# Within-chunk products of an SSD mixer: two heads in one PSUM bank instead of one

## The chip, the cores and the metric

The kernel runs on one core of one Trainium2 chip, as one program. The metric is the device time of an execution in microseconds (us). The core has a matrix engine (TensorE, PE in the profile; its weight loads are PEld), a vector engine (VectorE, DVE), an activation engine (ScalarE, ACT), a general engine (GpSimd, POOL) and a queue for transfers (SyncE, SP). Each engine takes its instructions strictly in the order of its program; engines wait for one another by semaphores.

## What is computed

Two layers of an encoder on 512 tokens of width 1024, in float32. Each layer has a mixing part (a pooling mixer, a bidirectional Mamba-2 mixer called SSD, gates, an output projection) and a gated feed-forward part. The change concerns the SSD mixer, cut from the reference to what matters:

```python
SSD_HEADS = 32; SSD_HEAD_DIM = 64; SSD_GROUPS = 4; SSD_STATE = 128; SSD_CHUNK = 128

def ssd_scan(xh, dt, a, bmat, cmat):            # one direction
    ...
    a_cum = jnp.cumsum(jnp.moveaxis(adt, 2, -1), axis=-1)
    seg = a_cum[..., :, None] - a_cum[..., None, :]
    decay = jnp.exp(jnp.where(lower, seg, -jnp.inf))
    scores = jnp.einsum('bclgn,bcsgn->bcgls', cc, bc)
    y_diag = jnp.einsum('bcghls,bcsghp->bclghp', scores[:, :, :, None] * decay, x)
    ...                                          # y_off: the states carried between chunks
    y = y_diag + jnp.moveaxis(y_off, 0, 1)

def bidirectional_ssd(...):
    y_f = ssd_scan(xh, dt[:, :, 0], a[0], bmat, cmat)
    y_b = fl(ssd_scan(fl(xh), fl(dt[:, :, 1]), a[1], fl(bmat), fl(cmat)))
    y = y_f + y_b + d_skip[:, None] * xh
```

The two directions of a head are summed as matrices: `exp` of the masked forward and backward segments, added, times the scores of the group, is one 128x128 matrix per chunk and head, and that matrix times the tokens of the head is `y_diag` of both directions.

## The kernel before, in words

**The main stream.** TensorE's order is written out in the program. Its main work is projections of the 512 tokens with streamed weights. Every float32 weight block is cut into two parts (`wh`, by a cast on ACT, line 90; `wl`, the rest, by a subtraction on DVE, line 91), and every product is three matmuls (lines 298 to 300, in `mm3`). The `wh` and `wl` tiles have three slots each, so a new block can be cast only when TensorE has finished with the block three before it. A projection writes a bank of PSUM from a pool of four (`bank_a`, tiles named `bc`, `xp`, `zp`, `up`, `g0p`, `spp` and so on).

**The background jobs.** The SSD mixer's small matmuls are generators (`Background`): after every few matmuls of the main stream, `bg.tick()` lets one of them put a piece of work into TensorE's order. They use a second pool of four banks (`bank_b`: `xt`, `btp`, `scp`, `stp`, `yop`, `ydp`, `ytp`). A bank is written again only when all that read it are done. The order on the other engines is made by a scheduler from the order in which the instructions were recorded and their priorities; the weights' casts have high priority.

**Units and groups.** Channels of SSD come in 8 units of 256 (4 heads each), 2 units to a group. A group `g` makes B and C (`bc`, then `bt` and `ct`, by a depthwise convolution: ACT reads the bank first, line 389, then DVE reads it four times, line 395, then a SiLU on ACT), their transposes and scores (`scp`, `sct`). A unit `u` makes its convolved tokens (`xp`, `xc`, transposed into `xtok`), its gate (`zp`, `zs`), the states (`stp`, `s`), the products with the states (`yop`, scaled into `yo` by DVE, added to `y` by POOL). When the unit's heads are done, `zs` takes `y`; after the second unit of a group the result is normalised, transposed (`ytp`), cut in two parts on ACT and DVE (`yth`, line 916; `ytl`, line 917), and projected (`spp`).

**The heads.** `heads_job` goes through the 32 heads. `decay(h)` issues a transfer of the two directions' cumulated rows from DRAM to all partitions on ACT's queue (line 756, tile `m`, 128x2x512), masks them on POOL (line 761), takes 8 exponentials of 128x128 on ACT (line 768) and adds the directions on DVE (line 769). Three `m` tiles are in flight. Then the head's matrix is multiplied by the scores on DVE (line 779), 8 matmuls with 64 columns of tokens each (line 786; each is two records in the profile) fill half of a bank `ydp`, and DVE adds it to `y` (line 792). Then `decay(h + 3)` is recorded.

Of the kernel before, what the change touches and what calls it, by code (L numbers as in the profile page):

```python
# [9 lines left out]
F32 = mybir.dt.float32  # L10
# [3 lines left out]
ALU = mybir.AluOpType  # L14
# [3 lines left out]
P = 128  # L18
T = 512
D = 1024  # L20
KD = D // P
NCH = T // P
# [3 lines left out]
ALPHA = (2 * NL) ** 0.25  # L26
EPS = 1e-5
# [9 lines left out]


class WeightStream:
    """Weights in the order in which TensorE takes them: a float32 block is loaded, then cut  # L40
    into two float32r parts whose sum is the block."""

    def __init__(self, nc, tc, pool, plan, ahead, raw_bufs, bufs):
        self.nc, self.tc, self.pool = nc, tc, pool
# [65 lines left out]


class Background:
    """Small pieces of TensorE work, put between the matmuls of the projections: one piece at
    most per tick; a piece says after how many ticks its successor's data can be there."""

    def __init__(self):
        self.jobs = []
# [104 lines left out]
def tile_hybrid_pool_ssd_convffn_encoder(  # L222
# [24 lines left out]
    nc = tc.nc  # L247
# [29 lines left out]
    after = triangle("after", -1, 1, -1)  # L277
# [63 lines left out]
    xq = []  # L341

    def feature_tiles(name, n):
        """n column tiles [128 features, 512 tokens] of the next weights times x."""
        tiles = []
        for i in range(n):
            wh, wl = ws.get()
            ps = bank_a(f"{name}{i}")
            for k in range(KD):
                mm3(ps[: wh.shape[2], :], wh[:, k, :], wl[:, k, :], xts["h"][:, k, :],  # L350
                    xts["l"][:, k, :], k == 0, k == KD - 1)
                if k % 2:
                    bg.tick()
            tiles.append(ps)
        return tiles

    def first_tiles(name, n, fresh=False):
        """The same, by halves of the tokens, with what is left of x's transposes in between."""
        tiles = [bank_a(f"{name}{i}") for i in range(n)]

        def transpose_to(left):
            while len(xq) > left:
                done = xq.pop(0)()
            return done

        got = [ws.get(0)] if fresh else []
        with ExitStack() as order:
            for ins in (last_load, *transpose_to(5)) if fresh else transpose_to(5):
                order.enter_context(tc.issue_after(ins.ins))
            got += [ws.get() for _ in range(n - len(got))]  # L370
        for t0, before in (
            (0, {(0, n - 1): 4, (1, n - 2): 2, (1, n - 1): 1}), (256, {(0, n - 1): 0})
        ):
            for k0 in (0, 4):
                for i in range(n):
                    if (k0 // 4, i) in before:
                        transpose_to(before[k0 // 4, i])
                    wh, wl = got[i]
                    t = slice(t0, t0 + 256)
                    for k in range(k0, k0 + 4):  # L380
                        mm3(tiles[i][: wh.shape[2], t], wh[:, k, :], wl[:, k, :],
                            xts["h"][:, k, t], xts["l"][:, k, t], k == 0, k == KD - 1)
                    bg.tick()
        return tiles

    def conv(dst, ps, taps, bias):
        """Centred depthwise convolution along the tokens; taps are per-feature columns."""
        mid = len(taps) // 2
        nc.scalar.activation(dst, ps, AF.Identity, bias=bias, scale=taps[mid])  # L389
        for j, tap in enumerate(taps):  # L390
# [7 lines left out]
            )  # L398

    def rsqrt(pool, v, name):  # L400
        """v ** -0.5 of positive columns: a guess from the bits, then Newton's iteration."""
        n = v.shape[1]
        i = pool.tile([P, n], I32, tag="rsi", name=f"rsi{name}", bufs=2)
        t = pool.tile([P, n], F32, tag="rst", name=f"rst{name}", bufs=2)
# [7 lines left out]
        return y  # L412

    def token_projection(l, name, src_h, src_l, kn, xcs, lnp, gt, bt, finish, final=False):
        """x <- LayerNorm(ALPHA * x + src @ w), token-major, by chunks of 128 tokens."""
        sts = []
        for c in range(NCH):
            n = 4 if final and c == NCH - 1 else 2
# [4 lines left out]
        warm = lnp.tile([P, 1], F32, tag="warm", name=f"warm{name}")  # L423

        def root(c, mv):
            """(variance + EPS) ** -0.5, with a step of Newton's iteration."""
            v = mv[:, 1:2]
            r = lnp.tile([P, 3], F32, tag="root", name=f"root{name}{c}", bufs=2)
            y, t = r[:, 0:1], r[:, 1:2]
# [5 lines left out]
            return y  # L435

        def pieces(half, c):
            """The columns of a half that are summed and finished together."""
            if final and half == 1 and c == NCH - 1:
                return [slice(0, 256), slice(256, 512)]  # L440
            return [slice(0, 512)]
# [91 lines left out]
            nc.gpsimd.memset(edge[:, gi, 1, t : t + 1], 1.0 / (w - t))  # L533

    for l in range(NL):
        # per-feature parameters as columns
        fw = ffn_conv_w[l].rearrange("j (t p) -> (j t) p", p=P)
        prows = [
            param_rows("pcw", [ssd_conv_w[l].rearrange("j (t p) -> (j t) p", p=P)]),
# [204 lines left out]
        heads_done = [0]  # L744

        def heads_job():
            """The masked decay matrices of the heads, both directions, and the products with
            them within the chunks of 128 tokens."""
            while not dts:
                yield 0  # L750
            nac = dts["nac"]
            ms = {}

            def decay(h):
                m = sp.tile([P, 2, T], F32, tag="m", name=f"m{l}_{h}", bufs=3)
                nc.scalar.dma_start(
                    m, acd[l].rearrange("(d h) t -> d h t", d=2)[:, h, :].partition_broadcast(P)
                )
                for d in range(2):
                    mv = m[:, d].rearrange("p (c t) -> p c t", c=NCH)  # L760
                    nc.gpsimd.affine_select(  # L761
                        out=mv, in_=mv, pattern=[[0, NCH], [1 - 2 * d, P]],
                        compare_op=ALU.is_ge, fill=NEG, base=0, channel_multiplier=2 * d - 1,
                    )
                    for c in range(NCH):
                        mc = m[:, d, c * P : (c + 1) * P]
                        col = d * 32 + h
                        nc.scalar.activation(mc, mc, AF.Exp, bias=nac[:, c, col : col + 1])  # L768
                nc.vector.tensor_tensor(m[:, 0], m[:, 0], m[:, 1], op=ALU.add)  # L769
                ms[h] = (m, bg.now)  # L770

            for h in range(3):
                decay(h)
            for h in range(32):
                u, hh = h // 4, h % 4
                m, start = ms.pop(h)
                while u // 2 not in grp or u not in ytiles or bg.now < start + (6 if h else 7):
                    yield 0
                nc.vector.tensor_tensor(m[:, 0], m[:, 0], grp[u // 2][2], op=ALU.mult)
                yield 2  # L780
                xtok, y = ytiles[u]
                ps = bank_b(f"ydp{l}_{h}")
                for c in range(NCH):
                    for q in range(2):
                        t0 = c * P + q * 64
                        nc.tensor.matmul(
                            ps[q * 64 : (q + 1) * 64, c * 64 : (c + 1) * 64],
                            lhsT=m[:, 0, t0 : t0 + 64],
                            rhs=xtok[:, c, hh * 64 : (hh + 1) * 64], start=True, stop=True,
                        )  # L790
                yv = y[:, :, hh * 64 : (hh + 1) * 64]
                nc.vector.tensor_tensor(
                    yv, yv, ps[:, :256].rearrange("p (c q) -> p c q", c=NCH), op=ALU.add
                )
                heads_done[0] = h + 1
                if h + 3 < 32:
                    decay(h + 3)
                yield 1

        def unit_job(u, xtok, zs, xjobs):  # L800
# [378 lines left out]
```

## Time and profile before

| | |
|---|---|
| runs of the kernel (3) | 1989.05 to 1992.81 us, median 1991.07 us |
| profiled execution, first to last instruction (span) | 1990.3 us |
| TensorE (PE) | 1954.0 us busy, 98% of the span, 10614 records |
| DVE | 1179.1 us busy, 59% |
| ACT | 947.9 us busy, 48% |
| POOL | 430.9 us busy, 22% |
| mean granted TensorE clock | 0.994 of full speed |

The span of the profiled execution lies 0.8 us under the median of the runs, so times of the profile can be set against the runs without a correction. TensorE's matmuls are pipelined: a matmul's record is longer than the distance to the next one's start, so what a piece of work costs TensorE is read from starts, not from durations. In the rows below, `x16` counts merged records, and the bracket at the end of a row gives the idle time of the engine ahead of it and what ended it. The layers are alike: layer 0's mixing part ends near 475 us, layer 1 begins near 995 us and repeats it.

### The profile page before, as it was taken

Reading aid. Unit: us, or ns where it says so; the run is one execution under the profiler, and the core shown is the slowest. Engines: PE = TensorE matmul, PEld = TensorE weight load, DVE = VectorE, ACT = ScalarE, POOL = GpSimd, SP = SyncE. Lnnn points to the kernel's source line nnn. Section 1 sums busy time; section 2 is a strip of 40 time slices with the busy share of each in tenths; the row PEclk is TensorE's granted clock in tenths of the full one; section 3 lists DMA queues with packets and bytes.
Section 4 is the critical chain, followed back from the end, with each engine's and each line's share of the span. In section 5 each row is a group of like instructions: output and inputs, shape, how many; then the busy total and the mean of one; then the engine's idle time right before and its main releaser. Section 6 shows DMA issues by size and latency. Waiting matters only on the chain.

```text
span 1990.3 us, 27038 instructions
## 1 busy us (share of the span) xinstructions
PE 1954.0 (98%) x10614; PEld 1643.9 (83%) x10614; DVE 1179.1 (59%) x1796; ACT 947.9 (48%) x1629; POOL 430.9 (22%) x456
## 2 busy tenths in 40 slices
PE   8999999999999999999999999999999999999998
PEld 7878798988888888888888888989888888888886
DVE  5568576775556655543475685667656566555334
ACT  4767666644332544431257776656443334444321
POOL 1344424241111111110003344252411111111000
PEclk9999999999999999999999999999999999999999
DMA  5443424233241323232325434443333413322321
GB/s 159 127 116 116 127 92 141 85 112 114 79 162 51 106 94 110 94 128 92 97 93 154 115 112 118 116 120 104 90 111 91 169 43 106 106 85 92 129 89 72
DMA packets 172160, 214.87 MB, mean 108 GB/s; under 512 B 6752, under 2 KB 127748, under 8 KB 172032
## 3 DMA queue, kind: packets, MB, share of 16 engines
q1 hardware_dynamic: 151376, 170.14, 26.9%
q10 hardware_dynamic: 17712, 34.08, 6.5%
q0 software_dynamic: 2944, 8.91, 1.4%
q8 instruction: 84, 1.38, 0.3%
q14 instruction: 44, 0.36, 0.1%
HBM read 208.66 MB, written 4.46 MB: 107 GB/s over the span
## 4 chain that ended last, share of the span: by engine, by line
PE 86%; issue 7%; ACT 2%; DVE 2%; POOL 1%; DMA 1%; SPq 0%; ACTq 0%; POOLq 0%; DVEq 0%
PE fg L300 7%; PE fg L299 7%; PE fg L298 7%; PE dp L298 4%; PE dp L299 4%; PE dp L300 4%; PE spp L298 3%; PE spp L299 3%; PE spp L300 3%; PE zp L298 3%; PE zp L299 3%; PE zp L300 3%; PE xp L298 2%; PE xp L299 2%; PE xp L300 2%
## 5 line engine op out<-in xcount | busy, mean ns | idle before, releaser
L91 DVE TENSOR_TENSOR wl<-wraw,wh 128x1024 fp32r<-128x1024 f32 (+1 forms) x318 | 395.8, 1246 | 394.9 <-ACT wh L90 393.6
L90 ACT CAST wh<-wraw 128x1024 fp32r<-128x1024 f32 (+1 forms) x318 | 328.4, 1035 | 434.2 <-PE dp L300 121.9
L300 PE MATMUL fg<-xthm,wl 128*128 128x512 f32 x640 | 249.0, 389 | 0.0
L298 PE MATMUL fg<-xthm,wh 128*128 128x512 f32 x640 | 249.0, 389 | 0.0
L299 PE MATMUL fg<-xtlm,wh 128*128 128x512 f32 x640 | 249.0, 389 | 0.0
L768 ACT ACTIVATE m<-m,nac 128x128 f32<-128x128 f32 x512 | 158.5, 389 | 53.1 <-POOL m L761 52.8
L1122 POOL TENSOR_TENSOR cvv<-cvv,cg 128x512 f32<-128x512 f32 x44 | 56.6, 1286 | 412.8 <-DVE cvv L395 382.0
L299 PEld LDWEIGHTS fg<-xtlm,wh 128*128 128x128 f32 x640 | 120.2, 188 | 25.0
L298 PEld LDWEIGHTS fg<-xthm,wh 128*128 128x128 f32 x640 | 120.2, 188 | 24.9
L300 PEld LDWEIGHTS fg<-xthm,wl 128*128 128x128 f32 x640 | 120.2, 188 | 24.8
L298 PE MATMUL dp<-wh,ah 128*128 128x512 f32 (+1 forms) x352 | 136.6, 388 | 0.0
L300 PE MATMUL dp<-wh,al 128*128 128x512 f32 (+1 forms) x352 | 136.4, 387 | 0.0
L299 PE MATMUL dp<-wl,ah 128*128 128x512 f32 (+1 forms) x352 | 136.4, 387 | 0.0
L761 POOL TENSOR_SCALAR_AFFINE_SELECT m<-m 128x512 f32<-128x512 f32 x128 | 95.0, 767 | 179.6 <-DMA m<-acd 136.8
L298 PE MATMUL spp<-yth,wh 128*128 128x512 f32 x256 | 110.3, 431 | 0.5 <-ACT yth L916 0.5
L876 POOL TENSOR_TENSOR y<-y,yo 128x256 f32<-128x256 f32 x96 | 85.9, 904 | 103.0 <-DVE yo L868 100.2
L299 PE MATMUL spp<-ytl,wh 128*128 128x512 f32 x256 | 101.2, 395 | 0.7 <-DVE ytl L917 0.7
L300 PE MATMUL spp<-yth,wl 128*128 128x512 f32 x256 | 101.1, 395 | 0.0
L395 DVE SCALAR_TENSOR_TENSOR xc<-xp,pcwc,xc 128x510 f32<-128x510 f32 (+1 forms) x128 | 95.2, 745 | 7.7 <-ACT xc L389 6.1
L1125 ACT CAST ah<-cvv 128x512 fp32r<-128x512 f32 x44 | 27.3, 621 | 147.2 <-POOL cvv L1122 147.2
L512 POOL TENSOR_TENSOR x<-x,lnb 128x512 f32<-128x512 f32 x15 | 20.2, 1345 | 325.7 <-DVE x L508 316.1
L769 DVE TENSOR_TENSOR m<-m 128x512 f32<-128x512 f32 x64 | 45.8, 716 | 64.2 <-ACT m L768 54.9
(347 smaller groups left out, 4779.1 us busy)
## 6 DMA issues: line engine op xcount, KB each, us to landing
wraw<-in_w_in_dram SPq DMA_DIRECT2D x56, 1024.0 KB, 5.5
wraw<-in_w_up_dram SPq DMA_DIRECT2D x44, 1024.0 KB, 5.1
m<-acd ACTq DMA_DIRECT2D x64, 512.0 KB, 4.9
wraw<-in_w_down_dram SPq DMA_DIRECT2D x20, 1024.0 KB, 5.1
wraw<-in_w_ssd_proj_dram SPq DMA_DIRECT2D x16, 1024.0 KB, 5.1
wraw<-in_w_in_dram SPq DMA_DIRECT2D x16, 512.0 KB, 5.5
wraw<-in_w_out_dram SPq DMA_DIRECT2D x8, 1024.0 KB, 5.3
xi<-in_x_dram SPq DMA_DIRECT2D x4, 512.0 KB, 6.9
```

The source lines that it names most:

```text
L90: self.nc.scalar.copy(hv, src)
L91: self.nc.vector.tensor_tensor(lv, src, hv, op=ALU.subtract)
L298: nc.tensor.matmul(ps, lhsT=ah, rhs=bh, start=first, stop=False)
L299: nc.tensor.matmul(ps, lhsT=ah, rhs=bl, start=False, stop=False)
L300: nc.tensor.matmul(ps, lhsT=al, rhs=bh, start=False, stop=last)
L395: nc.vector.scalar_tensor_tensor(dst[:, o0:o1], ps[:, o0 + s : o1 + s], tap, dst[:, o0:o1], op0=ALU.mult, op1=ALU.add,)
L761: nc.gpsimd.affine_select(out=mv, in_=mv, pattern=[[0, NCH], [1 - 2 * d, P]], compare_op=ALU.is_ge, fill=NEG, base=0, channel_multiplier=2 ...
L768: nc.scalar.activation(mc, mc, AF.Exp, bias=nac[:, c, col : col + 1])
L769: nc.vector.tensor_tensor(m[:, 0], m[:, 0], m[:, 1], op=ALU.add)
L876: nc.gpsimd.tensor_tensor(y[:, c, :], y[:, c, :], yo[:, d, :], op=ALU.add)
L1122: nc.gpsimd.tensor_tensor(cv, cv, cg, op=ALU.mult)
L1125: nc.scalar.copy(h, cv)
```

## The change

Heads are taken in pairs. A decay tile is made per direction: `m` (forward, four slots) and `mb` (backward, two slots), each 128x512 with a transfer of its own, so that a head has two transfers of 256 KB instead of one of 512 KB. Four heads are prepared ahead instead of three. A pair's two matrices are multiplied by the scores, then 16 matmuls (32 records) fill all 512 columns of one bank, and one addition takes the bank into `y`. Then the next pair but one is prepared. The pauses in ticks are 3 after the multiplications (2 before) and 9 instead of 7 for the first head. The diff also drops docstrings and one comment, which leave empty lines. Its core:

```diff
             def decay(h):
-                m = sp.tile([P, 2, T], F32, tag="m", name=f"m{l}_{h}", bufs=3)
-                nc.scalar.dma_start(
-                    m, acd[l].rearrange("(d h) t -> d h t", d=2)[:, h, :].partition_broadcast(P)
-                )
-                for d in range(2):
-                    mv = m[:, d].rearrange("p (c t) -> p c t", c=NCH)
+                m = sp.tile([P, T], F32, tag="m", name=f"m{l}_{h}", bufs=4)
+                mb = sp.tile([P, T], F32, tag="mb", name=f"mb{l}_{h}", bufs=2)
+                for d, t in enumerate((m, mb)):
+                    col = d * 32 + h
+                    nc.scalar.dma_start(t, acd[l][col : col + 1, :].partition_broadcast(P))
+                    mv = t.rearrange("p (c t) -> p c t", c=NCH)
                     nc.gpsimd.affine_select(
                         out=mv, in_=mv, pattern=[[0, NCH], [1 - 2 * d, P]],
                         compare_op=ALU.is_ge, fill=NEG, base=0, channel_multiplier=2 * d - 1,
                     )
                     for c in range(NCH):
-                        mc = m[:, d, c * P : (c + 1) * P]
-                        col = d * 32 + h
+                        mc = t[:, c * P : (c + 1) * P]
                         nc.scalar.activation(mc, mc, AF.Exp, bias=nac[:, c, col : col + 1])
-                nc.vector.tensor_tensor(m[:, 0], m[:, 0], m[:, 1], op=ALU.add)
+                nc.vector.tensor_tensor(m, m, mb, op=ALU.add)
                 ms[h] = (m, bg.now)
 
-            for h in range(3):
+            for h in range(4):
                 decay(h)
-            for h in range(32):
+            for h in range(0, 32, 2):
                 u, hh = h // 4, h % 4
-                m, start = ms.pop(h)
-                while u // 2 not in grp or u not in ytiles or bg.now < start + (6 if h else 7):
+                (m0, _), (m1, start) = ms.pop(h), ms.pop(h + 1)
+                while u // 2 not in grp or u not in ytiles or bg.now < start + (6 if h else 9):
                     yield 0
-                nc.vector.tensor_tensor(m[:, 0], m[:, 0], grp[u // 2][2], op=ALU.mult)
-                yield 2
+                for m in (m0, m1):
+                    nc.vector.tensor_tensor(m, m, grp[u // 2][2], op=ALU.mult)
+                yield 3
                 xtok, y = ytiles[u]
                 ps = bank_b(f"ydp{l}_{h}")
-                for c in range(NCH):
-                    for q in range(2):
-                        t0 = c * P + q * 64
-                        nc.tensor.matmul(
-                            ps[q * 64 : (q + 1) * 64, c * 64 : (c + 1) * 64],
-                            lhsT=m[:, 0, t0 : t0 + 64],
-                            rhs=xtok[:, c, hh * 64 : (hh + 1) * 64], start=True, stop=True,
-                        )
-                yv = y[:, :, hh * 64 : (hh + 1) * 64]
+                for j, m in enumerate((m0, m1)):
+                    for c in range(NCH):
+                        for q in range(2):
+                            t0 = c * P + q * 64
+                            nc.tensor.matmul(
+                                ps[q * 64 : (q + 1) * 64,
+                                   c * P + j * 64 : c * P + (j + 1) * 64],
+                                lhsT=m[:, t0 : t0 + 64],
+                                rhs=xtok[:, c, (hh + j) * 64 : (hh + j + 1) * 64],
+                                start=True, stop=True,
+                            )
+                yv = y[:, :, hh * 64 : (hh + 2) * 64]
                 nc.vector.tensor_tensor(
-                    yv, yv, ps[:, :256].rearrange("p (c q) -> p c q", c=NCH), op=ALU.add
+                    yv, yv, ps.rearrange("p (c q) -> p c q", c=NCH), op=ALU.add
                 )
-                heads_done[0] = h + 1
-                if h + 3 < 32:
-                    decay(h + 3)
+                heads_done[0] = h + 2
+                for n in (h + 4, h + 5):
+                    if n < 32:
+                        decay(n)
                 yield 1
```

The change moves instructions on every engine but SP, because the scheduler orders ACT, DVE and POOL anew and the jobs fall on other ticks. From the first head pair on, the heads stand earlier among the background pieces. Three places follow. The numbers behind a tile's name are group or unit, then head or column tile.

On ACT in layer 0, around the reading of the bank `bc_1_0` by the convolution of group 1's B (`bt_1`): before,

```order
L90 CAST wh_1143<-wraw_1141 128x1024
L768 ACTIVATE m_3_992<-m_3_992,nac_709 128x128 x2
L768 ACTIVATE m_4_1044<-m_4_1044,nac_709 128x128 x8
L756 DMA m_5_1102<-acd_89 128x2x512
L389 ACTIVATE bt_1_1126<-bc_1_0_975,pcbc,pcwc 128x512
L389 ACTIVATE ct_1_1133<-bc_1_1_1065,pcbc,pcwc 128x512
L756 DMA m_6_1177<-acd_89 128x2x512
L90 CAST wh_1223<-wraw_1141 128x1024
```

and in the changed kernel

```order
L767 ACTIVATE m_6_1156<-m_6_1156,nac_709 128x128 x4
L759 DMA mb_7_1176<-acd_89 128x512
L767 ACTIVATE mb_6_1157<-mb_6_1157,nac_709 128x128 x4
L767 ACTIVATE m_7_1175<-m_7_1175,nac_709 128x128 x2
L90 CAST wh_1363<-wraw_1361 128x1024
L767 ACTIVATE m_7_1175<-m_7_1175,nac_709 128x128 x2
L767 ACTIVATE mb_7_1176<-mb_7_1176,nac_709 128x128 x4
L389 ACTIVATE bt_1_1194<-bc_1_0_1005,pcbc,pcwc 128x512
L389 ACTIVATE ct_1_1201<-bc_1_1_1099,pcbc,pcwc 128x512
```

The reading of `bc_1_0` stood behind the exponentials of head 4 and two casts ahead of `wh_1275`, the cast that takes the slot freed by the last matmul of `xp_2_1` (the column tile of TensorE's stream right ahead of `zp_2_0`); now it stands behind the exponentials of head 7 and behind that same cast, which is `wh_1363` here, with 6 exponentials in between. In both kernels `zp_2_0` writes the bank that `bc_1_0` had.

On ACT in layer 0, around the reading of the first transposed result of group 0 (`ytp_0_0`) by the cut into `yth_0`: before,

```order
L90 CAST wh_1999<-wraw_1997 128x512
L768 ACTIVATE m_12_1871<-m_12_1871,nac_709 128x128 x5
L768 ACTIVATE m_13_1928<-m_13_1928,nac_709 128x128 x8
L736 ACT_TABLE_LOAD
L736 ACTIVATE zs_3_1620<-zp_3_0_1631 128x512
L736 ACTIVATE zs_3_1620<-zp_3_1_1741 128x512
L916 ACTIVATE yth_0_1679<-ytp_0_0_1958,pcbc 128x512
L90 CAST wh_2080<-wraw_2078 128x1024
```

and in the changed kernel

```order
L90 CAST wh_2021<-wraw_1962 128x1024
L767 ACTIVATE m_14_1905<-m_14_1905,nac_709 128x128 x3
L767 ACTIVATE mb_14_1906<-mb_14_1906,nac_709 128x128 x4
L767 ACTIVATE m_15_1924<-m_15_1924,nac_709 128x128 x4
L767 ACTIVATE mb_15_1925<-mb_15_1925,nac_709 128x128 x4
L736 ACT_TABLE_LOAD
L736 ACTIVATE zs_3_1720<-zp_3_1_1839 128x512
L920 ACTIVATE yth_0_1639<-ytp_0_0_1975,pcbc 128x512
```

On TensorE the four transposes `ytp_0` stood between matmuls of `up_0_1` and `g0p_0_0`, with other pieces among them; now all four stand in `up_0_0`, with 6 matmuls after each of the first three, and the next background piece is `xt_3_0`, 12 matmuls behind the fourth. `xt_3_0` writes the bank of `ytp_0_0` again. The cast `wh_2021` waits for the last use of the first part of `up_0_0`'s weights.

On DVE in layer 0, in the changed kernel, ahead of the scaling of `yop_1_1` into `yo_1_1`:

```order
L91 TENSOR_TENSOR wl_1368<-wraw_1361,wh_1367 128x1024
L395 SCALAR_TENSOR_TENSOR xc_2_1_1353<-xp_2_1_0_1270,pcwc,xc_2_1_1353 128x510
L395 SCALAR_TENSOR_TENSOR xc_2_1_1353<-xp_2_1_0_1270,pcwc,xc_2_1_1353 128x511
L91 TENSOR_TENSOR wl_1568<-wraw_1565,wh_1567 128x1024
L395 SCALAR_TENSOR_TENSOR xc_2_1_1353<-xp_2_1_0_1270,pcwc,xc_2_1_1353 128x511
L768 TENSOR_TENSOR m_10_1437<-m_10_1437,mb_10_1438 128x512
L395 SCALAR_TENSOR_TENSOR xc_2_1_1353<-xp_2_1_0_1270,pcwc,xc_2_1_1353 128x510
L768 TENSOR_TENSOR m_11_1456<-m_11_1456,mb_11_1457 128x512
L872 TENSOR_TENSOR yo_1_1_1579<-yop_1_1_1578,ef_704 128x512
```

Here `yop_1_1` and `yop_1_2`, which follow each other on TensorE 6 matmuls apart, have been given the same bank (in the kernel before they had two different ones), so `yop_1_2` waits for this `yo_1_1`, and `yo_1_1` for the addition of head 11, whose last exponential stands 18 instructions behind the first one of head 10 on ACT.

## Rows read from the trace of the kernel before

**Rows 1.** The page, part 1: busy time, share, instructions

```profile
PE 1954.0 (98%) x10614; PEld 1643.9 (83%) x10614; DVE 1179.1 (59%) x1796; ACT 947.9 (48%) x1629; POOL 430.9 (22%) x456
```

**Rows 2.** TensorE's waits, whole span: us in total, times, longest us

```profile
PE stp L835 <- POOL xw L818: 6.5, 4, 2.1
PE g0p L298 <- ACT zs L736: 3.0, 2, 1.9
...
PE ydp L786 <- ACT m L768: 0.8, 2, 0.4
PE spp L299 <- DVE ytl L917: 0.7, 2, 0.4
```

**Rows 3.** Timeline of TensorE around a head's products: start us, us, instruction

```profile
87.28 0.39 PE L300 MATMUL bc<-xthi,wl 128*128 128x512 f32 x1
87.60 0.69 PE L786 MATMUL ydp<-xtok,m 128*64 128x64 f32 x16
...
88.55 0.39 PE L299 MATMUL bc<-xtli,wh 128*128 128x512 f32 x1
```

**Rows 4.** Timeline of TensorE around four and eight transposes in a row

```profile
15.89 0.60 PE L305 MATMUL xtpi<-ident,xi 128*128 128x128 f32 x4
...
16.44 0.28 PE L299 MATMUL dbc<-xtli,wh 128*128 128x256 f32 x1
...
19.20 1.03 PE L305 MATMUL xtpi<-ident,xi 128*128 128x128 f32 x8
...
20.19 0.28 PE L299 MATMUL dbc<-xtli,wh 128*128 128x256 f32 x1
```

**Rows 5.** The tile m: duration ns min/median/max, and landing times

```profile
L761 POOL TENSOR_SCALAR_AFFINE_SELECT m<-m x128: 629/636/1715, 71.0 to 1418.6; 128x512 f32<-128x512 f32 x128
...
DMA to landing us min/median/max: 4.5/4.9/9.5
```

**Rows 6.** Timeline of ACT, 60 to 130 us

```profile
78.07 0.37 ACTq L756 DMA_DIRECT2D m<-acd  x1
78.09 3.31 ACT L768 ACTIVATE m<-m,nac 128x128 f32<-128x128 f32 x11
...
115.56 1.04 ACT L90 CAST wh<-wraw 128x1024 fp32r<-128x1024 f32 x1
```

**Rows 7.** Timeline of ACT, 104 to 106 us

```profile
104.79 0.76 ACT L389 ACTIVATE bt<-bc,pcbc,pcwc 128x512 f32<-128x512 f32 x1
```

**Rows 8.** Timeline of TensorE at the end of xp_2_1 and the start of zp_2_0

```profile
114.96 0.39 PE L299 MATMUL xp<-xtli,wh 128*128 128x512 f32 x1
...
115.41 0.28 PE L298 MATMUL zp<-wh,xthi 128*128 128x256 f32 x1
```

**Rows 9.** Timeline of DVE at the convolution of group 1's B and C

```profile
107.54 0.74 DVE L395 SCALAR_TENSOR_TENSOR bt<-bc,pcwc,bt 128x510 f32<-128x510 f32 x1
108.20 0.73 DVE L395 SCALAR_TENSOR_TENSOR ct<-bc,pcwc,ct 128x510 f32<-128x510 f32 x1
```

**Rows 10.** Groups by form on ACT: busy us, mean ns | idle before

```profile
L916 ACT ACTIVATE yth<-ytp,pcbc 128x512 fp32r<-128x512 f32 x32 | 20.9, 694 | 10.7 <-PE ytp L911 10.7
L736 ACT ACTIVATE zs<-zp 128x512 f32<-128x512 f32 x32 | 18.8, 593 | 1.8 <-PE zp L300 1.5
...
L736 ACT ACT_TABLE_LOAD x12 | 15.4, 1283 | 0.2
```

**Rows 11.** Groups by form on DVE: the same columns

```profile
L917 DVE SCALAR_TENSOR_TENSOR ytl<-ytp,pcbc,yth 128x512 fp32r<-128x512 f32 x32 | 23.4, 746 | 5.6 <-ACT yth L916 5.6
```

**Rows 12.** Windows: us, busy us (instructions) of PE, PEld, DVE, ACT, POOL, then PEclk

```profile
118.00:124.00 6.00, 3.38 (x25) 2.78 (x23) 5.48 (x7) 3.21 (x9) 2.72 (x2) 1.00 0.27 87
124.00:126.00 2.00, 1.31 (x5) 1.18 (x6) 0.75 (x1) 0.30 (x1) 2.00 (x2) 0.74 0.00 0
126.00:128.00 2.00, 2.00 (x11) 1.93 (x10) 1.08 (x2) 1.57 (x2) 2.00 (x3) 0.50 0.00 0
128.00:130.00 2.00, 2.00 (x27) 1.78 (x26) 0.42 (x1) 1.73 (x3) 0.66 (x2) 0.90 0.01 4
```

## The prediction

> **What bounds the kernel now.** I read the busy shares first, then TensorE's waits, then its timeline. TensorE is busy 98% of the span and ACT 48% [rows 1], so a change pays only by taking work or waits out of TensorE's order, and costs only by putting them in. The waits by releaser show how little is left: four groups make nearly all that TensorE waits for inside the two mixing parts, 6.5 us for `xw`, 3.0 for a gate `zs` on ACT, 0.8 for a head's exponentials, 0.7 for `ytl`, 11.0 us for both layers [rows 2]. The shares hide what decides: ACT serves TensorE in two ways, it casts weights and reads PSUM banks, and it does both in one order with the exponentials. The reader should look for what stands in front of a bank's reading.
>
> **What the products cost.** A head's 16 records take TensorE from the matmul at 87.28 to the second matmul behind them at 88.55, 1.27 us, of which two ordinary steps of 0.23 (half of the 0.45 us between the starts at 114.96 and 115.41) are not theirs: 0.81 us [rows 3, 8]. Nothing in the trace has 32 such records in a row. Bounds: nothing is saved by joining two groups, or at most one entry (0.32 less 0.23) and as much again at the exit, 0.2 us for each of 32 pairs, 6.4 us. The nearest rows are groups of four and eight transposes: 0.55 us from the first record to the second matmul behind four, 0.99 behind eight [rows 4], so the second four cost 0.44; the first four cost 0.55 less one step of 0.12, 0.43. Joining saves nothing there, so I take 0. The 64 additions that become 32 wider ones are DVE's and TensorE does not wait for them; the cover is the many ticks until `zs` needs `y`, and were it gone each pair would show one addition of some 0.7 us (a like 512-column read of a bank is 0.75 [rows 11]).
>
> **What the waits of before do.** The pairs run earlier in TensorE's order, and the waits of [rows 2] sit at places that are rearranged: `stp_1_1` stands behind the new stall below, which gives POOL time; `ytp_3` is now spread between matmuls. I take all 11.0 us as gone (bounds 0 and 11.0).
>
> **The new stalls.** All three follow one pattern: TensorE reaches a bank whose reader stands on ACT or DVE behind exponentials that were recorded for the next pairs.
>
> Stall 1, `zp_2_0`. It needs the bank of `bc_1_0`, read by one ACT instruction and four DVE taps. Before, ACT read it at 104.79 [rows 7], DVE began at 107.54 [rows 9], and `zp_2_0` began at 115.41 without a wait [rows 8]. In the new order ACT's reading stands behind a cast that waits for the last use of `xp_2_1`'s weights, the matmul started at 114.96; that cast began at 115.56 [rows 6, 8], 0.60 us later, and cannot begin earlier in the new kernel. Behind it: the cast 1.04, six exponentials at 3.31/11 = 0.30 each, 1.8, the reading 0.76, then seven DVE taps, since B's and C's alternate at 0.66 us, 6 x 0.66 + 0.74 = 4.7 [rows 6, 7, 9]. From 115.56 these 8.3 us end at 123.9, 8.5 us after TensorE would have begun `zp_2_0` at 115.41. It hangs on no transfer; if the exponentials ahead are late it grows.
>
> Stall 3, `xt_3_0`. It needs the bank of `ytp_0_0`, and the reading stands behind the cast `wh_2021`, released by the last use of `up_0_0`'s first weights. From the start of that matmul: 0.60 to the cast, the cast 1.04, 15 exponentials 4.5, a table load 1.28, `zs` 0.59, `yth` 0.69, `ytl` 0.75, together 9.45 [rows 6, 8, 10, 11]. TensorE does in that time two matmuls (0.45), four transposes (0.43) and 12 matmuls (2.75), 3.6 us. Stall: 5.8 us.
>
> Stall 2, `yop_1_2`. It shares a bank with `yop_1_1`, whose reading stands on DVE behind head 11. From TensorE's restart at `zp_2_0`, ACT has 15 exponentials (4.5), three table loads (3.8), three SiLUs and a copy (0.6 each, as `zs`), 10.7 us; then 16 exponentials, two casts and a reading, 7.7; then two DVE instructions of at most 0.75: 19.9 us. TensorE has until then 96 matmuls of half width (0.12 each, 11.5), 12 full ones (2.8) and pieces worth some 6.9 (a pair of heads 1.6; the others as four or eight transposes): 21.2. So the lower bound is no stall. The upper: head 10's transfer is issued behind a copy that itself waits for TensorE, and its landing (4.9) and mask (0.64) [rows 5] lie wholly in the chain: 25.4 less 21.2, 4.2 us. That issues run ahead of the engine's work is visible: the transfer at 78.07 went out while 11 exponentials that stand before it were still to run [rows 6]. But POOL masks head 10 behind two multiplications of states that wait for the same copy. I take 3.5, near the upper end.
>
> **The clock.** The granted clock was 1.00 until 124, then 0.74, 0.50 and 0.90 in three windows of 2 us [rows 12]; 0.50 is the 1.2 GHz level, and ahead of it TensorE was busy for 3.38 of 6 us, in the `stp` waits. The loss is (0.26 + 0.50 + 0.10) x 2 = 1.7 us. Each layer has one such dip in its mixing part, and its wait goes. I expect one behind stalls 1 and 3 each and none, or one, behind stall 2: (4 - 2) x 1.7 = 3.4 us more, bounds 0 and 6.8.
>
> **What is hidden.** The 64 more transfers add issues on ACT's queue, and a few table loads at 1.28 us each stand in ACT's order; ACT is idle half of the time and waits elsewhere, so outside the three places I cost them at nothing. Without that cover each lands in a stall's sum at its full duration.
>
> **The sum.** Per layer 8.5 + 3.5 + 5.8 = 17.8; for two layers 35.6; less 11.0; plus 3.4; plus 0 for the joining: 28.0 us. The profiled execution is 1990.3 us, 0.8 under the runs' median; 1991.07 + 28.0 = 2019 us, slower by 1.4%.
>
> **Rivals.**
>
> Faster. The old waits go (11.0), both dips go (3.4), joining saves its bound (6.4), and no new stall appears: 1970 us; without the joining 1977. It decides from the point where the last DVE tap of `bt_1` is done before `xp_2_1` ends, that is if ACT reads `bc_1_0` before the cast. For it speaks that ACT is idle half of the time; against it that this cast begins 0.2 us after TensorE's tile ends, and six exponentials and the reading stand behind it in a fixed order. Chance 0.05.
>
> Only stall 1. Stall 2 is at its lower bound, and the results' readings come in time, because ACT reaches the exponentials of heads 14 and 15 before the cast's slot is free: 2 x 8.5 less 11.0, with as many dips as before: +6, 1997 us. For it speaks that transfers run ahead; against it the order behind `wh_2021`. Chance 0.08.
>
> Transfers in the chain. A head now has two transfers, and only two `mb` slots exist, so a backward tile's transfer waits for the addition two heads earlier and is issued from ACT's own order. If at each of the three places one more landing and mask falls into the chain, each stall grows by 4.9 + 0.64 = 5.5 us: 6 x 5.5 = 33 us more, 2052 us. For it speaks that masks waited for landings often, with a median of 4.9 us [rows 5]; against it the issue at 78.07 that ran ahead. A halved transfer would land sooner only if the landing goes with the bytes. The Trainium skill, in "DMA: Bandwidth & Descriptors", section "Anatomy of one DMA — SWDGE (gpsimd) path", gives each transfer about 2.0 us that no size changes, mostly the confirmation of its end, and says that a wait is served on the issuing queue before the transfer is sent: twice as many transfers are then twice as much fixed time, and a wait for a slot holds up all behind it. By its fit a 256 KB transfer would take 2.6 us (an estimate from that page), and the three stalls would grow by 3.2 instead of 5.5 us, to 2039. The trace has no 256 KB transfer of this kind. Chance 0.09.
>
> No change. The stalls come out at about 5.5 us a layer, so that the waits that go and the stalls that come cancel. Chance 0.03.
>
> **How the numbers follow.** The forecast has 0.75. The range goes from 1999, which is the forecast with stall 2 and the extra dips at nothing and stall 3 at half, to 2042, the forecast with all bounds up and part of the transfers in the chain. About 0.2% (4 us) is what a measurement of this kernel can tell from no change. Faster by more than that: 0.05. Within it: 0.03. Slower: 0.92, from the forecast, stall 1 alone and the transfers.
>
> **What the profile would show.** Right: TensorE's waits of `zp` for DVE's taps on `bt`, near 8.5 us and once a layer; of `xt` for `ytl` near 6; of `yop` for `yo` up to 4; granted clock at 0.50 behind the first and third; the `stp` wait for `xw` gone; a pair's 32 records at 1.6 us. Wrong: no wait at `zp_2_0`, or `bt`'s reading on ACT ahead of the cast in time; a pair well under 1.6 us, which would make the joining worth something; waits of `ydp` for `m`, which would mean that four heads ahead are too few. The forecast fails most easily on ACT's arrival: I take ACT to be at each cast when TensorE releases it.

## The result, and the profile after

The changed kernel takes 2022.47 us (median of 4 runs, 2018.71 to 2025.72), the kernel before beside it 1991.94 us (4 runs, 1989.05 to 1996.57): a ratio of 1.0153, with a 95% interval of 1.0133 to 1.0172. The profiled execution has a span of 2018.9 us, 28.6 us more than that of before.

The page's part 1, which answers to [rows 1]:

```profile
PE 1948.8 (97%) x10614; PEld 1648.6 (82%) x10614; DVE 1184.4 (59%) x1764; ACT 958.0 (47%) x1633; POOL 432.7 (21%) x456
```

TensorE is busy for 5.2 us less than before, with the same number of records, and the span is longer all the same. So the change took work out of TensorE's stream and put waiting in. TensorE's waits by releaser (us in total, times, longest), which answer to [rows 2]:

```profile
PE zp L298 <- DVE bt L395: 16.3, 2, 8.2
PE xt L576 <- DVE ytl L921: 11.0, 2, 5.5
PE ytp L915 <- DVE y L795: 10.8, 2, 5.4
PE yop L866 <- DVE yo L872: 8.8, 2, 4.6
```

All groups of [rows 2] are gone. In their place stand four waits, each once a layer, 46.9 us in all. The rows for `zp`, `xt` and `yop` are the prediction's stalls 1, 3 and 2; the third row, `ytp` for an addition into `y`, was not forecast.

**Stall 1.** The timeline of ACT from the cast on:

```profile
114.97 1.04 ACT L90 CAST wh<-wraw 128x1024 fp32r<-128x1024 f32 x1 [0.69 <-PE xp L299]
...
115.93 0.40 ACT L767 ACTIVATE m<-m,nac 128x128 f32<-128x128 f32 x1
...
116.81 0.97 ACT L767 ACTIVATE mb<-mb,nac 128x128 f32<-128x128 f32 x3
117.69 0.76 ACT L389 ACTIVATE bt<-bc,pcbc,pcwc 128x512 f32<-128x512 f32 x1
```

DVE behind it, and TensorE:

```profile
117.87 0.69 DVE L768 TENSOR_TENSOR m<-m,mb 128x512 f32<-128x512 f32 x1 [0.59 <-ACT mb L767]
...
122.44 0.74 DVE L395 SCALAR_TENSOR_TENSOR bt<-bc,pcwc,bt 128x510 f32<-128x510 f32 x1
```

```profile
114.78 0.40 PE L300 MATMUL xp<-xthi,wl 128*128 128x512 f32 x1
123.33 0.55 PE L298 MATMUL zp<-wh,xthi 128*128 128x256 f32 x1 [8.16 <-DVE bt L395]
```

ACT stood idle for 0.69 us until TensorE had finished with the weights; then the cast, six exponentials and the reading of `bc_1_0` follow without a gap, and no transfer's landing lies among them. DVE's last tap ends at 123.18 and TensorE goes on.

**Stall 3** has the same form. ACT's timeline from the cast behind `up_0_0` to the reading of `ytp_0_0`:

```profile
192.98 1.05 ACT L90 CAST wh<-wraw 128x1024 fp32r<-128x1024 f32 x1 [0.67 <-PE up L299]
193.94 0.99 ACT L767 ACTIVATE m<-m,nac 128x128 f32<-128x128 f32 x3
...
197.17 1.26 ACT L767 ACTIVATE mb<-mb,nac 128x128 f32<-128x128 f32 x4
198.45 1.28 ACT L736 ACT_TABLE_LOAD   x1
199.74 0.60 ACT L736 ACTIVATE zs<-zp 128x512 f32<-128x512 f32 x1
200.24 2.42 ACT L920 ACTIVATE yth<-ytp,pcbc 128x512 fp32r<-128x512 f32 x4
```

**Stall 2**, ACT's timeline at the exponentials of head 10, whose sum with the backward direction `yo_1_1` stands behind:

```profile
141.22 1.28 ACT L767 ACTIVATE m<-m,nac 128x128 f32<-128x128 f32 x4 [3.68 <-POOL m L761]
```

Here ACT waited for POOL's mask. What held the mask up shows in POOL's timeline:

```profile
137.62 1.13 POOL L847 TENSOR_TENSOR s<-s,tot 128x512 f32<-128x512 f32 x1 [10.38 <-ACT s L845]
139.55 1.04 POOL L847 TENSOR_TENSOR s<-s,tot 128x512 f32<-128x512 f32 x1 [0.80 <-DVE s L854]
140.54 0.64 POOL L761 TENSOR_SCALAR_AFFINE_SELECT m<-m 128x512 f32<-128x512 f32 x1
```

The mask follows two multiplications of states without a gap. Its transfer does not hold it up. The issue is in ACT's timeline, and the trace has 3.4 us from there to the landing, so the tile was there at 137.3, 3.2 us before the mask began:

```profile
133.95 0.33 ACTq L759 DMA_DIRECT2D m<-acd  x1
```

**The stall that was missed.** DVE's timeline ahead of `ytp_0_0`, and TensorE's:

```profile
182.38 0.69 DVE L768 TENSOR_TENSOR m<-m,mb 128x512 f32<-128x512 f32 x1 [4.09 <-ACT m L767]
...
184.85 0.68 DVE L768 TENSOR_TENSOR m<-m,mb 128x512 f32<-128x512 f32 x1
185.45 0.68 DVE L795 TENSOR_TENSOR y<-y,ydp 128x512 f32<-128x512 f32 x1
```

```profile
186.19 1.12 PE L915 MATMUL ytp<-ident,zs 128*128 128x128 f32 x4 [5.41 <-DVE y L795]
```

The addition that empties the bank of heads 10 and 11 stands on DVE behind the additions of heads 12 and 13, and the first of these waited 4.09 us for ACT's exponentials. `ytp_0_0` writes that bank. ACT had itself been idle until DVE's taps on a tile `xc` were done, and then took two table loads and a SiLU ahead of the exponentials:

```profile
178.37 1.28 ACT L570 ACT_TABLE_LOAD   x1 [4.66 <-DVE xc L395]
```

**A pair's products**, TensorE's timeline, to be set beside [rows 3]:

```profile
92.24 0.40 PE L300 MATMUL bc<-xthi,wl 128*128 128x512 f32 x1
92.57 1.15 PE L787 MATMUL ydp<-xtok,m 128*64 128x64 f32 x32
93.65 0.50 PE L298 MATMUL bc<-xthi,wh 128*128 128x512 f32 x1
93.98 0.39 PE L299 MATMUL bc<-xtli,wh 128*128 128x512 f32 x1
```

From the matmul ahead to the second one behind it are 1.74 us; less two ordinary steps of 0.23 that is 1.28 us for 32 records. Two groups of 16 cost 2 x 0.81 = 1.62 us before. A joined pair saves 0.33 us (from the unrounded times), and 32 pairs 10.6 us.

**The clock**, windows of 2 us, columns as in [rows 12]: one window at the 1.2 GHz level for each stall. The whole stretches at that level last 10.2, 3.4, 3.4 and 6.8 us in this layer and begin within the stall or up to 1 us behind it.

```profile
124.00:126.00 2.00, 2.00 (x11) 2.00 (x11) 2.00 (x4) 0.93 (x2) 2.00 (x4) 0.50 0.00 0
...
152.00:154.00 2.00, 2.00 (x7) 1.54 (x6) 2.00 (x3) 0.96 (x2) 1.55 (x3) 0.50 0.48 173
...
186.00:188.00 2.00, 1.81 (x7) 1.62 (x8) 1.26 (x2) 1.40 (x2) 1.80 (x1) 0.50 0.82 255
...
202.00:204.00 2.00, 2.00 (x7) 1.73 (x8) 2.00 (x4) 1.62 (x4) 0.00 (x0) 0.50 0.01 5
```

The account by spans: new waits +46.9, old waits -11.0, joining -10.6, together +25.3 of the measured +28.6. The 3.3 us that remain do not measure the clock. In all, the granted clock is at the 1.2 GHz level for 55.0 us, of which 15.2 fall into TensorE's waits, against 22.1 and 0.5 before. Half of what lies outside the waits is 19.9 against 10.8 us, so the clock costs some 9 us more (an estimate from these times), and the account comes out some 6 us too long. Either TensorE's own work shrank by more than the joining's 10.6, or the estimate for the clock is too high; experiments 1 and 4 come back to it.

### The profile page after: what moved, and what is told of

The parts are those of the page before. It is cut to its first block, busy times and chain, and to the rows that moved or that the text cites. A ratio compares the mean times of both kernels' runs of the same rounds, so it can differ in the third digit from the quotient of the medians.

```text
span 2018.9 us, 27136 instructions
## 1 busy us (share of the span) xinstructions
PE 1948.8 (97%) x10614; PEld 1648.6 (82%) x10614; DVE 1184.4 (59%) x1764; ACT 958.0 (47%) x1633; POOL 432.7 (21%) x456
## 4 chain that ended last, share of the span: by engine, by line
PE 82%; issue 8%; ACT 4%; DVE 4%; POOL 1%; DMA 1%; ACTq 0%; SPq 0%; POOLq 0%; DVEq 0%
PE fg L300 7%; PE fg L298 7%; PE fg L299 7%; PE dp L298 4%; PE dp L299 4%; PE dp L300 4%; PE spp L298 3%; PE spp L300 3%; PE spp L299 3%; PE xp L298 2%; PE xp L299 2%; PE xp L300 2%; PE zp L298 2%; PE yop L866 2%; PE zp L300 2%
## 5 line engine op out<-in xcount | busy, mean ns | idle before, releaser
L880 POOL TENSOR_TENSOR y<-y,yo 128x256 f32<-128x256 f32 x96 | 90.2, 947 | 83.0 <-DVE yo L872 80.0
L767 ACT ACTIVATE mb<-mb,nac 128x128 f32<-128x128 f32 x256 | 84.0, 393 | 46.0 <-POOL mb L761 45.6
L767 ACT ACTIVATE m<-m,nac 128x128 f32<-128x128 f32 x256 | 83.1, 393 | 37.0 <-POOL m L761 36.4
L768 DVE TENSOR_TENSOR m<-m,mb 128x512 f32<-128x512 f32 x64 | 48.0, 750 | 68.4 <-ACT m L767 33.7
```

The source lines that it names most:

```text
L768: nc.vector.tensor_tensor(m, m, mb, op=ALU.add)
L880: nc.gpsimd.tensor_tensor(y[:, c, :], y[:, c, :], yo[:, d, :], op=ALU.add)
```

## The experiments

Theory A, from the traces: TensorE reaches banks whose readers stand, on ACT or DVE, behind exponentials and additions that were recorded early; the joining itself is a gain. Rivals: the divided tiles make the stalls (B); the joining is worth nothing (C, the prediction's zero). The kernel before, run beside them, had medians of 1991.3 to 1991.6 us.

**1. The decays recorded later** (`late`).

```diff
                 heads_done[0] = h + 2
-                for n in (h + 4, h + 5):
-                    if n < 32:
-                        decay(n)
+                yield 4
+                if h + 4 < 32:
+                    decay(h + 4)
+                yield 3
+                if h + 5 < 32:
+                    decay(h + 5)
```

> The changed kernel with its products, tiles and transfers as they are; only the recording of the decays is moved: four ticks pass after a pair's products before head h+4 is prepared, and three more before head h+5. Theory A (order): the four stalls of the changed kernel (zp for bt, xt for ytl, ytp for y, yop for yo, 46.9 us in the table of waits) exist because the readers of banks stand behind exponentials and additions that were recorded too early; they go, with their clock dips, and the 32 joined groups keep what they save (0.35 us a pair, 11 us): 1970 to 1985 us, likeliest 1977, with those four waits below 5 us together. Theory B (tiles): the two tiles, 128 transfers and two slots for the backward direction make the stalls; nothing of that is changed: 2010 to 2025 us.

Measured: 1971.07 us, ratio 0.9899 (0.9885 to 0.9913). The same tiles, transfers and joined groups are now faster than the kernel before. Its waits:

```profile
PE zp L299 <- DVE wl L91: 4.8, 3, 2.4
PE xt L576 <- DVE ytl L924: 3.4, 3, 2.0
...
PE spp L299 <- DVE ytl L924: 0.7, 2, 0.3
```

All four stalls are gone. ACT reads `bc_1_0` 19 us earlier than in the changed kernel:

```profile
98.54 0.78 ACT L389 ACTIVATE bt<-bc,pcbc,pcwc 128x512 f32<-128x512 f32 x1
```

The 3.4 us that `xt` still waits for `ytl` are at other places (the longest at 270.2). The span is 48.7 us shorter than that of the changed kernel. The four stalls less these waits account for 38.0 us. The mean granted clock rises from 0.986 to 0.996: outside the waits the 1.2 GHz level lasts 15.1 instead of 39.8 us, worth some 12 us at half speed (an estimate from these times), which closes this account to within 2 us. B is out as the main cause.

**2. Only the divided tiles** (`split`): the kernel before with the tiles and transfers of the change, `m` with three slots, `mb` with two.

```diff
-                m = sp.tile([P, 2, T], F32, tag="m", name=f"m{l}_{h}", bufs=3)
+                m = sp.tile([P, T], F32, tag="m", name=f"m{l}_{h}", bufs=3)
+                mb = sp.tile([P, T], F32, tag="mb", name=f"mb{l}_{h}", bufs=2)
...
```

> The kernel before, single heads and three heads ahead, with only the tiles of the change: a forward tile (three slots) and a backward tile (two slots) with a transfer each, so 128 transfers of 256 KB. Theory A (order): the recording order is that of before, so no stall of the changed kernel appears: 1990 to 2000 us, likeliest 1995. Theory B (tiles): most of the 30 us appears: 2008 to 2025 us, with waits of zp, xt or yop of several us.

Measured: 1997.39 us, ratio 1.0035 (1.0023 to 1.0046). The tiles cost some 6 us, not 30; two waits stand out, one that was 6.5 us before [rows 2] and a new one, and neither is one of the four:

```profile
PE stp L834 <- POOL xw L817: 9.1, 4, 4.2
PE xt L576 <- ACT xc L570: 6.2, 2, 3.1
```

**3. Pairs with the tile of before** (`three`), three slots, the next two heads prepared at once.

```diff
+                m = sp.tile([P, 2, T], F32, tag="m", name=f"m{l}_{h}", bufs=3)
...
+                for n in (h + 3, h + 4):
```

> Pairs with joined products, but one tile and one transfer of 512 KB for both directions and three slots, as before: heads h+3 and h+4 are prepared after a pair. Theory A (order): two heads are still recorded at once, so long waits of TensorE remain, though at other places, less 11 us for the joining: 1992 to 2012 us. Theory B (tiles): without the divided tiles the stalls are gone and the joining shows: 1972 to 1985 us.

Measured: 2002.78 us, ratio 1.0061 (1.0048 to 1.0074). Without divided tiles there is a long wait too, at another place:

```profile
PE stp L840 <- POOL xw L823: 24.9, 5, 12.0
```

**4. The joined group parted** (`late_unjoin`): experiment 1 with one tick between the halves of a pair and a pause of two instead of three ahead of it. Its trace has 62 groups of products instead of 32.

```diff
-                yield 3
+                yield 2
...
                 for j, m in enumerate((m0, m1)):
+                    if j:
+                        yield 1
```

> As the version with late decays, but one tick is put between the two heads of a pair, so that other matmuls stand between two groups of 16 records; one addition as in the changed kernel, and the pause ahead is one tick shorter. Theory A: the joining saves 0.35 us a pair, so it is 11 us slower than the version with late decays, up to 18 if a wait appears where the ticks have moved. Theory C (the prediction's zero): the joining saves nothing and it is within 4 us of it.

Measured: 1991.11 us, ratio 0.9999 (0.9991 to 1.0008), 20.0 us over experiment 1 and so a little over what A allowed. The waits:

```profile
PE g0p L298 <- ACT u L968: 8.6, 2, 4.3
...
PE spp L298 <- ACT yth L925: 4.0, 4, 2.2
...
PE spp L299 <- DVE ytl L926: 2.3, 4, 0.8
```

These are 14.9 us against the 8.9 shown for experiment 1, so the moved ticks cost 6.0. Thirty more groups at 0.33 us are 9.9. Together 15.9 of the 17.9 us between the two spans; 2 us stay open. C is out. All traces together say the same. Take from each span TensorE's waits and half of the time at the 1.2 GHz level outside them: 1949.7 to 1952.7 us are left in the four kernels with groups of 16 records (before, `split`, `ahead4`, `late_unjoin`) and 1937.2 to 1940.6 in the nine with joined groups, about 12 us less (an estimate from these traces).

**5. Four heads ahead, one at a time** (`ahead4`): single heads with 16 records, divided tiles, `m` with four slots.

```diff
...
-            for h in range(3):
+            for h in range(4):
                 decay(h)
...
-                if h + 3 < 32:
-                    decay(h + 3)
+                if h + 4 < 32:
+                    decay(h + 4)
```

> Single heads with 16 records a group as before, but the divided tiles with four forward slots, and four heads prepared ahead instead of three; one head is recorded at a time. Theory A1 (being four heads ahead is what puts the exponentials in front of the banks' readings): waits of zp for bt and of xt for ytl of 4 to 8 us in each layer, 2008 to 2022 us. Theory A2 (it is the pairs, two heads recorded at once): no wait above 4 us, 1994 to 2003 us, as the version with divided tiles and three heads ahead (1997).

Measured: 2024.33 us, ratio 1.0161 (1.0147 to 1.0175). Against experiment 2 there is one more head ahead, with its slot, and nothing else, and it is 27 us more, a little beyond A1's range. `u` is the copy by which the pooling mixer empties a bank on ACT:

```profile
PE g0p L298 <- ACT u L958: 15.1, 2, 7.9
PE zp L298 <- DVE bt L395: 14.8, 2, 7.4
```

So pairs are not needed for stall 1. It comes with the fourth head ahead. The wait of `xt` for `ytl`, which A1 named too, is not there; this run does not bring stall 3 back.

**6. One stall cured by priority**, `bt` and `ct`'s convolutions in the one kernel (`bc`), the cut of `ytp` in the other (`yt`), with nothing else changed:

```diff
+            with tc.high_priority():
+                conv(bt, tiles[0], xbc_taps(16 + g), xbc_bias(16 + g))
...
```

```diff
+                    with tc.high_priority():
                         nc.scalar.activation(yth[:, f, :], ps, AF.Copy, scale=gcol)
...
```

> The changed kernel with one thing more: the convolutions of B and C (ACT's reading of the bank and the DVE taps) have the weights' high priority. Theory A (the prediction's stall 1): zp no longer waits for bt (16.3 us). If nothing else was late under that cover, it is 2000 to 2006 us; if POOL's xw is, which TensorE needs a few matmuls later and which is made from tokens that ACT copies behind the same exponentials, a wait of stp of 5 to 8 us takes its place, 2010 to 2022 us. I take the second for likelier.

> The changed kernel with one thing more: the cut of the transposed result into yth and ytl has the weights' high priority, so that its reading of the bank no longer stands behind the exponentials of heads 14 and 15. Theory A (the prediction's stall 3, chain on ACT): the waits of xt (11.0 us) go with a dip each (1.7): 2005 to 2013 us. Theory D (the bank's reading is late for another reason, or the next piece waits as long): 2017 to 2024 us.

Measured: 2018.96 us, ratio 1.0135 (1.0121 to 1.0149), and 2027.00 us, ratio 1.0177 (1.0163 to 1.0191): neither is told apart from the changed kernel's 1.0153 for the better. In each, the wait that was treated is gone. The waits of `bc`:

```profile
PE stp L843 <- POOL xw L826: 16.8, 4, 8.8
PE xt L576 <- DVE ytl L925: 13.9, 2, 7.0
PE ytp L919 <- ACT s L849: 12.7, 2, 6.3
```

and of `yt`:

```profile
PE pop L298 <- ACT ph L988: 10.6, 2, 5.3
...
PE spp L298 <- ACT acc L940: 3.8, 2, 2.2
```

In `bc` the 16.3 us of `zp` give way to 16.8 at `stp`, as its second case had it, but with 8.8 us at most instead of 5 to 8; in `yt` the 11.0 us of `xt` give way to 10.6 at `pop` and 3.8 at `spp`. In `yt` ACT was made to wait for TensorE's transposes, and the exponentials and `u`, whose result becomes `ph`, stand behind that (`u` is read at 206.18 there, at 202.52 in the changed kernel):

```profile
190.93 0.69 ACT L921 ACTIVATE yth<-ytp,pcbc 128x512 fp32r<-128x512 f32 x1 [2.73 <-PE ytp L915]
```

Neither theory had `yt` above 2024 us. Stall 3's place and chain were right; the idea that a cured stall gives back its length was wrong in both.

**7. Which part of the delay helps**: four ticks and both heads at once (`both4`), and no delay with five ticks between the heads (`spread5`).

```diff
+                yield 4
                 if h + 4 < 32:
                     decay(h + 4)
-                yield 5
                 if h + 5 < 32:
                     decay(h + 5)
```

(Lines with - stand in `spread5` alone, lines with + in `both4` alone.)

> Half of the version with late decays (1971.1 us): four ticks pass after a pair's products, then both next heads are prepared at once. If the delay is what counts (the readings of banks are recorded first), 1975 to 1990 us, with no wait of zp for bt above 2 us. If the spreading is what counts, 2000 to 2020 us.

> The other half: head h+4 is prepared right behind the products, as in the changed kernel, and head h+5 five ticks later. If the delay is what counts, the readings still stand behind the first head's exponentials: 2000 to 2020 us. If the spreading counts, 1978 to 1995 us. By the order of the instructions I expect the second, with a few waits of 3 to 4 us left (xt, g0p).

Measured: `both4` 1978.60 us, ratio 0.9939 (0.9925 to 0.9952); `spread5` 1993.58 us, ratio 1.0011 (1.0002 to 1.0020). `both4` lies in the range that was given for the delay, `spread5` in that for the spreading, so both count. Against 2022.47 the delay gives back 44 us, more than the loss of 30.5, and the spreading 29, nearly all of it. What `spread5` still waits for is more than the 3 to 4 us that were expected, up to 5.6 us at `g0p` for `u`.

**8. Other places in the region** (`late5`: 5 and 3 ticks; `late6`: 6 and 2).

```diff
-                yield 4
+                yield 6
...
-                yield 3
+                yield 2
```

> As the version with late decays (1971.1 us), with five ticks instead of four ahead of head h+4. Theory A: a head at a time, later than the readings, is a region and not one lucky place: 1968 to 1978 us, no wait of zp for bt, ytp for y or yop for yo above 2 us. If the gain hangs on one place: above 1980 us.

> As the version with late decays, with six ticks ahead of head h+4 and two more ahead of head h+5: a third place in the same region. Theory A: 1968 to 1978 us; faster than 1971.1 only if the waits of zp for wl (4.8 us) and xt for ytl (3.4) go too, 1963 to 1967.

Measured: `late5` 1976.00 us, ratio 0.9918 (0.9905 to 0.9932); `late6` 1967.89 us, ratio 0.9884 (0.9869 to 0.9899), the fastest version here. `late5` lies in the region's range and `late6` at its lower edge. But `late5` has a wait of `ytp` for `y` of up to 2.5 us (4.9 in all), over the 2 us that were set, and within the region the place still makes a difference of some 8 us. In `late6` the waits of `zp` and `xt` of experiment 1 are gone; what its mixing parts still wait for is small:

```profile
PE spp L299 <- DVE ytl L924: 2.1, 4, 0.8
PE spp L298 <- ACT gp L998: 2.0, 2, 1.0
PE ytp L918 <- DVE ytl L924: 1.8, 2, 0.9
```

## Why the prediction was right, and where it was not

The time was forecast as 2019 us and measured as 2022.47, inside the range. The cause forecast, readers of banks that stand behind work prepared ahead, is the one that the experiments confirm. But the joining (-10.6 us against 0), a stall that was missed (+10.8), the clock (some +9 against 3.4) and stall 2 (8.8 against 7.0) were off, and their errors cancelled but for the 6 us that the account leaves open, so the closeness of the total is in good part luck. The lower end of the range is no help either: 1999 does not follow from the terms named for it, which give 1991.07 + 2 x (8.5 + 2.9) - 11.0 = 2003.

- **Stall 1**: forecast 8.5 us a layer, measured 8.2, by the chain that was named; only the addition of head 7 stands on DVE ahead of the taps, and the cast began 0.43 us after its matmul's start (114.54 in the trace) instead of 0.60. Right.
- **Stall 3**: forecast 5.8, measured 5.5, with the same chain. Right.
- **Stall 2**: forecast 3.5, measured 4.2 and 4.6, about the upper bound, but not for its reason. That bound put head 10's landing (4.9) and mask wholly into the chain. The landing was over some 3.2 us before the mask began. ACT's 3.68 us of idle time were POOL's two multiplications of states, with an addition of DVE's between them, and the mask behind them: the order that the prediction named last and gave no price. The place was right; that the size came near is luck.
- **The old waits**: all 11.0 us gone. Right. Experiment 6 agrees with the reason given for `stp`: where stall 1 is cured alone, `stp` waits again.
- **"Joining saves nothing there, so I take 0"**: wrong. It saves 10.6 us, beyond the bound of 6.4. Transposes were a poor stand-in for these narrow products, and the bound counted one step at each end while a group's ends cost more: 0.33 us a pair. The prediction named "a pair well under 1.6 us" as what would show this; it is 1.28.
- **"TensorE does not wait for them"** (the additions into `y`): wrong. The cover was looked for where `zs` needs `y`, but the same addition also frees the bank of the products, and `ytp_0_0` takes that bank: 5.4 us a layer, 10.8 in all. The rule used for the other three stalls, to ask what stands ahead of a bank's reader, was not applied to this reader.
- **The clock**: mis-sized. Forecast were four dips at 1.7 us, +3.4 us over the two of before and at most +6.8. There are eight in the mixing parts, one with each of the four stalls in both layers, and five of them last 6.8 or 10.2 us instead of 3.4. The estimate above gives some +9 us.
- **What is hidden**: the divided tiles were put at nothing. Alone they cost 6 us (experiment 2), mostly in the waits shown there; why those grew is not shown. In the changed kernel that is not a term of its own.
- **Rivals.** "Faster" did not happen, but experiments 1 and 8 come to its figure of 1970 (1971, 1976 and 1968) once the decays are recorded later. "Only stall 1" is out, since the other stalls came. "Transfers in the chain" needed a landing in each stall and had it in none of the four. The landings, from part 6 of the profile's page:

```profile
m<-acd ACTq DMA_DIRECT2D x64, 256.0 KB, 3.8
mb<-acd ACTq DMA_DIRECT2D x64, 256.0 KB, 3.7
```

Half the bytes land in 3.8 us instead of 4.9 [rows 5]. The Trainium skill's "DMA: Bandwidth & Descriptors", section "Anatomy of one DMA — SWDGE (gpsimd) path", gives 2.6 us by its fit for GpSimd's path (an estimate from that page); the measured 3.8 on ACT's queue decides. A part that does not go with the bytes is there, as the Trainium skill has it; a straight line through 3.8 and 4.9 puts it at 2.7 us (an estimate from the two medians) instead of 2.0.

The engine that decides is ACT, busy for 47% of the span. The Trainium skill's "PSUM — Partial Sum Buffer", section "Engine vs sequencer instructions", says that its queue is strictly first in, first out, and the trace agrees: a reading that can go at 98.54 us with the decays recorded later went at 117.69 here because of what was recorded ahead of it.

What stays open: why the cures by priority move a wait to exactly the places they do, what shrank TensorE's own work by some 5 us more than the joining (before and after lie at opposite ends of the two groups of experiment 4), and about 2 us of experiment 4.

## What to carry to other kernels

Preparing work further ahead is not free on an engine that also empties PSUM banks: its order decides when a bank is free again, so record prefetched work behind the readings that TensorE needs soon, and spread it, before giving up the change that needed it. For each bank that is written again, list every reader and what stands ahead of it on its engine, the last reader of the very thing that was changed included. Do not price a stall by curing it alone: in both trials here the engine was still late, and the next reader paid. When a wait on an engine has a transfer behind it, look at whether the transfer had landed before blaming it.

## What was not expected of the hardware

Thirty-two records of narrow matmuls in a row cost 1.28 us where two groups of 16 cost 1.62: entering and leaving such a group has a price of some 0.33 us beyond the records, more than the 0.2 that the neighbours' steps had suggested. Experiment 4 agrees with it to within 2 us over 30 groups.
